# Borders between mixer and MLP in a four-layer fp32 trunk: norm root on other engines, combinations moved, out-projection reordered

## The chip, the cores and the metric

The kernel runs on one core of one Trainium2 chip. The metric is the device time in microseconds (us) of one execution. The kernel before has a median of 2815.55 us over 3 runs (2807.36 to 2817.22).

## The reference, cut to what matters

Four residual layers act on a stream of 528 positions of width 1024. The mixers are, in order, gated DeltaNet (layer 0), differential attention (layer 1), RG-LRU (layer 2) and DeltaNet again (layer 3). An MLP with squared ReLU stands behind each.

```
def rmsnorm(x, w):
    y = xf * lax.rsqrt(jnp.mean(xf * xf, axis=-1, keepdims=True) + EPS)
    return y * w

for layer in range(DEPTH):
    u = rmsnorm(h, norm_mix_w[layer])
    y = (gated_deltanet, diff_attention, rglru_block)[layer % 3](u, ...)   # ends in: o @ w_out
    h = h + keep * y
    u = rmsnorm(h, norm_mlp_w[layer])
    h = h + keep * (jnp.square(jax.nn.relu(u @ w1)) @ w2)
h = rmsnorm(h, final_norm_w)
```

## The kernel before, in words

**Layout.** The stream lies transposed: tile `h[d]` holds channels 128 d to 128 d + 127 on the partitions and 528 positions along the free axis, d = 0 to 7. A product takes two halves of 264 positions (256 where only the output positions are left).

**Precision.** Every fp32 operand of a large product is split in a high part `hi` and a rest `lo`, and three products of the 1-pass format are summed: hi·hi, hi·lo and lo·hi (`part`, L372). A weight tile of 1024 columns is split by `wsplit` (L296): ScalarE makes `hi` (L305); `lo` is either a VectorE subtraction (L307, mode "v") or ScalarE's negative of `hi` (L309) to which a DMA from the GpSimd queue adds the weight from HBM (L310, mode "d"). `LO_ENG` (L46) names the mode for the two tiles of a row of weights; a name that is not in it has "dd". Seven slots of the pool `wp` hold the split tiles, so a tile is made when an earlier one has been used up.

**The norm.** The weight-scaled stream is multiplied first and the factor 1/sqrt(mean square) is applied when a product leaves PSUM. `norm_sq` (L417) squares `h[d]` on ScalarE (L429) and adds it to `ssum` on GpSimd (d = 1 to 6) or VectorE (d = 7), L430. `norm_finish` (L435) sums over the partitions with TensorE (`ones`), takes mean and EPS on VectorE (L442), the power -1/2 on GpSimd (L444, tile `rt`), spreads it over the partitions with TensorE into PSUM, and copies it to `rb` on ScalarE (L450).

**The border from mixer to MLP.** `out_proj` (L600) multiplies the eight head outputs by the output weight and adds the result to `h[d]` (L612). For DeltaNet and attention it makes two passes over d: heads 0 to 3, then heads 4 to 7; before each pass `drain` waits until those heads have been emitted. In the last pass `mlp_prep` (L454) follows each d: two ScalarE passes (L461, L462), a VectorE rest (L463) and `norm_sq`. Then `mlp` (L575) opens two plain columns of the first MLP weight with the first seven d (`open`), finishes the norm, and calls `mlp_combine` (L467) for the four pairs of d: six VectorE subtractions (L477) and two ScalarE casts (L480, L483) each, which build the operands of a seven-product scheme used for the other columns (`w1_pair`, L530).

**PSUM.** Eight banks: 3 in the pool `d` (large products), 5 in the pool `c` (all else). `psd` (L273) hands some `d` requests to the pool `c` where `self.wide` says so.

**What sets the order.** Background work (heads, gates, scans) is written as generators, which `tick` advances between matmuls by a model time; `t_img` in `dn_core` (L876) is such a time, at which a head may use matrices that a DMA brings back. The program runs under `schedule_with_timeline_sim=True`: at compile time a planner orders each engine's instructions by its own cost estimates, with program order as the priority, and `keep_in_program_order` pins an instruction. On the chip every engine and queue runs its own list in order.

**Other lines touched.** `lru_scan` (L1159) begins with four square roots on ScalarE (L1162). `run` (L1254) ends with the final norm: L1273 multiplies eight tiles by `rb`, three on GpSimd and five on VectorE, and L1274 writes them out.

Of the kernel before, what the change touches and what calls it, by code (L numbers as in the profile page):

```python
# [11 lines left out]
AF = mybir.ActivationFunctionType  # L12
ALU = mybir.AluOpType
# [4 lines left out]
NT = 8  # L18
# [24 lines left out]

LATS = [1.7] * 8 + [1.1]

LO_ENG = {"w2": "vd", "lru_in": "vd", "lru_out": "vd", "lru_gate": "vd"}  # L46

PRODS = (11, 21, 2, 3, 4, 1, 22)
OUT_PARTS = {"dn_out": (4, 4), "da_out": (4, 4), "lru_out": (8,)}


def out_order(name):

    o, n0 = [], 0
    for n in OUT_PARTS[name]:
        o += [(d, k) for d in range(8) for k in range(n0, n0 + n)]
        n0 += n
    return o


def unit_list(layers=LAYERS):
# [85 lines left out]
class K:  # L147
    def __init__(self, ctx, tc, hT, wts, cols, bc, cst, onehot, relb, out, layers):
# [22 lines left out]
        self.rb = per([128, TP], "rb")  # L171
        self.ones = per([128, 1], "ones")
        self.half = per([128, 1], "half")
        self.nhalf = per([128, 1], "nhalf")
        self.NS, self.NL = 34, 7
        self.sp = pool("sp", bufs=self.NS)
# [16 lines left out]
        nc.vector.memset(self.ssum, 0.0)  # L193
        nc.vector.memset(self.ones, 1.0)
        nc.vector.memset(self.half, 0.5)
        nc.vector.memset(self.nhalf, -0.5)
        self.ident = self.cst[:, CST["ident"]:CST["ident"] + 128]
        self.dimg = [self.drp.tile([2 * NC * (CB + 1), CB], F32, name=f"dimg{i}", bufs=1) for i in range(2)]
# [218 lines left out]
    def norm_sq(self, d, dve=False):  # L417
        nc = self.nc
        a = self.t0
        if dve:  # L420
            i = self.getl()
            nc.vector.tensor_tensor(self.S(i), self.h[d], self.h[d], ALU.mult)
            (nc.vector if d > 4 else nc.gpsimd).tensor_tensor(self.ssum[:, :T], self.ssum[:, :T], self.S(i), ALU.add)
            return
        if d == 0:
            nc.scalar.activation(self.ssum[:, a:T], self.h[d][:, a:], AF.Square)
        else:
            i = self.getl()
            nc.scalar.activation(self.S(i)[:, a:], self.h[d][:, a:], AF.Square)  # L429
            (nc.vector if d == NT - 1 else nc.gpsimd).tensor_tensor(self.ssum[:, a:T], self.ssum[:, a:T], self.S(i)[:, a:], ALU.add)  # L430

    def us(self):
        return self.u

    def norm_finish(self):  # L435

        nc = self.nc
        ps = self.psc()
        for c in range(NC):
            self.mmul(ps[:C, c:c + 1], lhsT=self.ssum[:, c * C:(c + 1) * C], rhs=self.ones, start=True, stop=True)  # L440
        ms = self.small([C, NC], "ms")
        nc.vector.tensor_scalar(ms, ps[:C, :NC], 1.0 / D, EPS, ALU.mult, ALU.add)  # L442
        rt = self.small([C, NC], "rt")
        nc.gpsimd.tensor_tensor(rt, ms, self.nhalf[:C].broadcast_to([C, NC]), ALU.pow)  # L444
        for c0, m in GR:
            pb = self.psc()
            for c in range(m):
                self.mmul(pb[:, c * C:(c + 1) * C], lhsT=rt[:, c0 + c:c0 + c + 1].broadcast_to([C, 128]),
                                 rhs=self.ident[:C, :C], start=True, stop=True)
            nc.scalar.copy(self.rb[:, c0 * C:(c0 + m) * C], pb[:, :m * C])  # L450
        return rt


# [121 lines left out]
    def mlp(self, l, next_prep, early=None):  # L575
        nc = self.nc
        self.open([("w1p", l, 0), ("w1p", l, 1)], self.us(), NT - 1)
        self.norm_finish()
        for p in range(NT // 2):
            self.mlp_combine(p)  # L580
        G = 32 // HG
        for g in range(G):
            xs = [] if g else self.w1_plain(l)
            for f in range(0 if g else 2, HG, 2):
                xs += self.w1_pair(l, g * HG + f, f == HG - 2)
            if g == 1 and early:
                self.spawn(early())
            self.wide = (0, 2, 4, 5, 7)
            self.open([("w2", l, d, g) for d in range(2)], xs, HG - 2)
            for d in range(NT):  # L590
                def ev(ps, t0, w):
                    h = self.h[d][:, t0:t0 + w]
                    nc.vector.tensor_tensor(h, h, ps, ALU.add)  # L593

                self.mm(("w2", l, d, g), xs, ev)
                if g == G - 1:
                    next_prep(d)
            self.wide = None

    def out_proj(self, name, slot, xs, l, part=None):  # L600

        nc = self.nc
        order = out_order(name)
        parts = OUT_PARTS[name]
        if part is None:
            part = len(parts) - 1
        n0, n = sum(parts[:part]), parts[part]
        if part == len(parts) - 1:
            self.ut, self.U = [], []
        for d in range(NT):  # L610
            def ev(ps, t0, w):
                nc.vector.tensor_tensor(self.h[d][:, t0:t0 + w], self.h[d][:, t0:t0 + w], ps, ALU.add)  # L612

            ws = []
            for k in range(n0, n0 + n):
                j, i = divmod(order.index((d, k)), 8)
                if i == 0:
                    self.ow = self.unit((name, slot, j))
                ws.append(tuple(x[:, i * 128:(i + 1) * 128] for x in self.ow))
            self.mmu(ws, [tuple(self.R(a) for a in xs[k]) for k in range(n0, n0 + n)], ev)  # L620
            if part == len(parts) - 1:
                self.mlp_prep(d, l * 8)


    def conv(self, x, y, wname, base, step, bias=None):
# [21 lines left out]
    def deltanet(self, slot, l, last):  # L647
# [45 lines left out]
        for h in range(8):  # L693
# [2 lines left out]
            hi, lo = self.get(True), self.get(True)  # L696
            xs.append((hi, lo))
            gates.append(self.spawn(self.dn_gate(heads[h], z, t, hi, lo), 0.7))
        n = 0
        for p, k in enumerate(OUT_PARTS["dn_out"]):  # L700
            n += k
            self.drain(*gates[:n])
            self.out_proj("dn_out", slot, xs, l, p)
        self.lat = 1.6

    def dn_beta(self, slot, xba, beta, ngc, negc, gd, tri):
# [68 lines left out]
    def dn_core(self, slot, l, h, cv, st, beta, ngc, negc, gd, mneg, ba):  # L775
# [97 lines left out]
        TM, TT = self.L(TMi, CB), self.L(TTi, CB)  # L873
        nc.sync.dma_start(TM[:CB], img(im, 0))
        nc.sync.dma_start(TT[:CB], img(im, NC * (CB + 1) * CB))
        t_img = self.now + 4.0  # L876
        yield 0.2

        vti = self.getl()
# [138 lines left out]
    def diffattn(self, slot, l, last):  # L1018
# [13 lines left out]
        self.open([("da_in", slot, 0), ("da_in", slot, 8)], us, NT - 1)  # L1032
        self.norm_finish()
        xs, gens = [None] * 8, []
        for h in range(8):
            q, k, v = self.get(), self.get(), self.get()

# [4 lines left out]
            self.mm(("da_in", slot, 8 + h), us, self.evac_rb(self.S(k)))  # L1042
            self.mm(("da_in", slot, 16 + h), us, self.evac_rb(self.S(v)))
            gens.append(self.spawn(self.da_core(h, xs, q, k, v, self.vs, nlam), 0.5))
        n = 0
        for p, k in enumerate(OUT_PARTS["da_out"]):
            n += k
            self.drain(*gens[:n])
            self.out_proj("da_out", slot, xs, l, p)

    def da_tiles(self, ts, q, k, E, Em, vt, on, so, nlam):
        nc = self.nc
# [106 lines left out]
    def lru_scan(self, fs, hs, xr, sg):  # L1159
        nc = self.nc  # L1160
        for f in fs:
            nc.scalar.activation(self.S(hs[f][0]), self.S(hs[f][0]), AF.Sqrt, scale=0.0625)  # L1162
        yield 0.5
        for f in fs:
            tr, ti, a = hs[f]
# [88 lines left out]
    def run(self):  # L1254
# [8 lines left out]
        for i, (kind, slot, l) in enumerate(L):  # L1263
# [3 lines left out]
                self.mlp(l, lambda d: self.norm_prep(d, "mix", nxt), self.bias_vectors if L[i + 1][0] == 1 else None)  # L1267
            else:
                self.mlp(l, self.final_prep)
        self.norm_finish()  # L1270
        for d in range(NT):
            o = self.S(self.fin[d])[:, NM:]
            (nc.gpsimd if d % 3 == 1 else nc.vector).tensor_tensor(o, o, self.rb[:, NM:T], ALU.mult)  # L1273
            nc.sync.dma_start(self.out[:, d, :], o)  # L1274

    def final_prep(self, d):
        self.norm_sq(d)
# [10 lines left out]
def layout(i, layers=LAYERS):  # L1288
# [10 lines left out]
    for n, j, u in ((n, j, u) for n, us in enumerate(rows) for j, u in enumerate(us)):  # L1299
# [14 lines left out]
            dst[:] = blk(i["mlp_w1"][u[1]], 0, u[2])  # L1314
        elif u[0] == "w2":
            dst[:] = blk(i["mlp_w2"][u[1]], u[3], u[2])
        elif u[0] in OUT_PARTS:
            w = i[u[0][:-4] + "_w_out"][u[1]]
            for j, (d, k) in enumerate(out_order(u[0])[8 * u[2]:8 * u[2] + 8]):
                dst[:, j * 128:(j + 1) * 128] = w[k * 128:(k + 1) * 128, d * 128:(d + 1) * 128]  # L1320
# [42 lines left out]
```

## Time and profile before

| | |
|---|---|
| median of 3 runs | 2815.55 us |
| profiled execution: its own time | 2808.51 us |
| profiled execution: span, first to last instruction | 2806.7 us |
| TensorE (PE) busy | 2685.4 us, 96% of the span |
| VectorE (DVE), ScalarE (ACT), GpSimd (POOL) busy | 60%, 52%, 26% |
| mean granted TensorE clock | 0.976 of full speed |

TensorE sets the time: what can be saved is its idle time and the time for which it ran at the lower clock. A row of a timeline gives the start and the length in us and, in brackets, how long the engine stood idle before and what released it. PEclk is the granted clock as a share of full speed.

### The profile page before, as it was taken

To read this page: it belongs to the slowest core of one execution; us is meant where nothing else is said; L and a number is where in the kernel's file an instruction comes from. 1 tells how busy PE (TensorE), PEld (TensorE's weight loads), DVE (VectorE), ACT (ScalarE), POOL (GpSimd) and SP (SyncE) were. 2 spreads that over 40 slices of the span, in tenths; PEclk is the share of its full clock that TensorE was granted. 3 is DMA by queue.
4 is the path that set the end of the run, shared out by engine and by line. 5 is a ranking of instruction groups with operands and counts; after the bars stand their busy time and mean duration, and the time that the engine had idled before them with its cause. 6 is when DMAs were issued, how large, how long until landed. Compare 5 with 4: busy or idle time off the path is not lost.

```text
span 2806.7 us, 54609 instructions
## 1 busy us (share of the span) xinstructions
PE 2685.4 (96%) x22080; PEld 2606.7 (93%) x22080; DVE 1674.3 (60%) x3841; ACT 1461.1 (52%) x3024; POOL 720.2 (26%) x984
## 2 busy tenths in 40 slices
PE   7899999999999999999999999999999999899997
PEld 7899898999998887999999999999999988799997
DVE  5755447656734445776566766776376553567763
ACT  4566555444545555543456854444566564544443
POOL 2655522101121112111122121111236453311112
PEclk9999999999999999999999999999999999999998
DMA  7755453354465443343454434433677454344333
GB/s 200 161 124 119 87 134 92 99 162 134 130 145 124 100 105 91 104 123 106 121 148 124 128 97 122 143 106 100 161 166 161 101 112 99 83 136 128 121 98 106
DMA packets 128866, 343.84 MB, mean 123 GB/s; under 512 B 72789, under 2 KB 73213, under 8 KB 103397
## 3 DMA queue, kind: packets, MB, share of 16 engines
q10 hardware_dynamic: 38496, 212.61, 22.0%
q0 software_dynamic: 28224, 102.77, 21.2%
q1 hardware_dynamic: 61892, 24.96, 3.7%
q8 instruction: 173, 2.83, 0.4%
q14 instruction: 81, 0.66, 0.1%
HBM read 331.99 MB, written 11.01 MB: 122 GB/s over the span
## 4 chain that ended last, share of the span: by engine, by line
PE 78%; issue 6%; DMA 5%; DVE 4%; POOL 4%; ACT 3%; DVEq 0%; ACTq 0%; POOLq 0%; SPq 0%
PE d L218 41%; PE c L218 35%; DMA lo<-in_wts_dram 2%; PE c L222 2%; POOL rt L444 1%; DVE op L307 1%; DMA s<-dimg 1%; DMA s<-gd 1%; POOL s L863 1%; DMA sa<-s 1%; POOL s L864 1%; ACT lo L309 0%; DMA gd<-l 0%; DVE l L539 0%; DMA dimg<-s 0%
## 5 line engine op out<-in xcount | busy, mean ns | idle before, releaser
L218 PE MATMUL c<-s,hi 128*128 128x264 f32 (+1 forms) x2816 | 522.0, 284 | 0.1
L218 PE MATMUL d<-uh,hi 128*128 128x264 f32 (+1 forms) x1584 | 468.5, 296 | 10.2 <-DVE s L642 10.1
L218 PE MATMUL d<-s,hi 128*128 128x264 f32 (+1 forms) x2432 | 467.9, 289 | 7.9 <-ACT s L400 2.0
L218 PE MATMUL d<-ul,hi 128*128 128x264 f32 (+1 forms) x1584 | 462.8, 292 | 0.0
L218 PE MATMUL d<-uh,lo 128*128 128x264 f32 (+1 forms) x1584 | 461.9, 292 | 0.4 <-DMA lo<-in_wts_dram 0.4
L218 PEld LDWEIGHTS c<-s,hi 128*128 128x128 f32 x2816 | 435.9, 188 | 1.4 <-issue 1.1
L310 POOL DMA_DIRECT2D lo<-in_wts_dram x196 | 173.9, 887 | 982.7 <-ACT lo L309 696.3
L218 PEld LDWEIGHTS d<-s,hi 128*128 128x128 f32 x2432 | 385.1, 192 | 13.6 <-issue 2.3
L218 PE MATMUL c<-s,lo 128*128 128x264 f32 (+1 forms) x1408 | 394.6, 284 | 1.9 <-DMA lo<-in_wts_dram 1.7
L309 ACT ACTIVATE lo<-hi 128x1024 fp32r<-128x1024 f32 x196 | 207.7, 1060 | 351.1 <-PE d L218 244.2
L305 ACT CAST hi<-raw 128x1024 fp32r<-128x1024 f32 x278 | 288.0, 1041 | 127.4 <-PE c L218 78.8
L218 PE MATMUL d<-s,lo 128*128 128x264 f32 (+1 forms) x1216 | 349.4, 288 | 3.6 <-DMA lo<-in_wts_dram 3.5
L218 PEld LDWEIGHTS d<-uh,hi 128*128 128x128 f32 x1584 | 306.4, 193 | 19.2 <-DVE s L642 13.7
L218 PEld LDWEIGHTS d<-uh,lo 128*128 128x128 f32 x1584 | 305.5, 193 | 5.2 <-issue 3.2
L218 PEld LDWEIGHTS d<-ul,hi 128*128 128x128 f32 x1584 | 306.0, 193 | 2.6 <-issue 1.6
L305 ACT CAST op<-raw 128x512 fp32r<-128x512 f32 x300 | 180.9, 619 | 168.7 <-PE d L218 100.3
L218 PEld LDWEIGHTS c<-s,lo 128*128 128x128 f32 x1408 | 263.5, 188 | 3.4 <-DMA lo<-in_wts_dram 3.1
L307 POOL TENSOR_TENSOR op<-raw,op 128x512 fp32r<-128x512 f32 x60 | 114.8, 1913 | 546.7 <-ACT op L305 407.0
L218 PEld LDWEIGHTS d<-s,lo 128*128 128x128 f32 x1216 | 232.9, 192 | 5.9 <-DMA lo<-in_wts_dram 4.2
L218 PE MATMUL d<-s,op 128*128 128x264 f32 (+1 forms) x1716 | 228.2, 284 | 0.0
L218 PEld LDWEIGHTS d<-s,op 128*128 128x128 f32 x1716 | 216.4, 188 | 0.0
L593 DVE TENSOR_TENSOR h<-h,c 128x264 f32<-128x264 f32 (+1 forms) x172 | 73.1, 425 | 229.3 <-PE c L218 228.9
(260 smaller groups left out, 5577.8 us busy)
## 6 DMA issues: line engine op xcount, KB each, us to landing
raw<-in_wts_dram ACTq DMA_DIRECT2D x197, 1024.0 KB
lo<-in_wts_dram POOLq DMA_DIRECT2D x196, 512.0 KB, 5.9
s<-dimg SPq DMA_DIRECT2D x32, 245.0 KB
sa<-s SPq DMA_DIRECT2D x16, 245.0 KB
s<-gd ACTq DMA_DIRECT2D x14, 265.0 KB
vs<-vd SPq DMA_DIRECT2D x8, 327.5 KB
h<-in_hT_dram SPq DMA_DIRECT2D x8, 264.0 KB
s<-vs SPq DMA_DIRECT2D x8, 264.0 KB
```

Source lines behind the costliest of these rows:

```text
L218: return self.nc.tensor.matmul(out, lhsT=lhsT, rhs=rhs, start=start, stop=stop)
L222: return self.nc.tensor.transpose(out, in_, ident)
L305: nc.scalar.copy(hi, src)
L307: lo_eng.tensor_tensor(lo, src, hi.bitcast(F32), ALU.subtract)
L309: nc.scalar.activation(lo, hi.bitcast(F32), AF.Copy, scale=-1.0)
L310: nc.gpsimd.dma_start(lo, dram, accum_op=ALU.add)
L444: nc.gpsimd.tensor_tensor(rt, ms, self.nhalf[:C].broadcast_to([C, NC]), ALU.pow)
L593: nc.vector.tensor_tensor(h, h, ps, ALU.add)
L863: nc.gpsimd.tensor_tensor(t, bt[:, j, j + 1:, None].broadcast_to([NB, r, j]), X[:, None, j, :j].broadcast_to([NB, r, j]), ALU.mult)
L864: nc.gpsimd.tensor_tensor(X[:, j + 1:, :j], X[:, j + 1:, :j], t, ALU.subtract)
```

## The change

The root of the norm has a second form, taken at the four MLP borders: a square root on ScalarE, then reciprocal and one Newton step on VectorE. `mlp_combine` for pairs 0 to 2 is called inside `out_proj`. The steps of the out-projection follow a list: heads 0 to 3 for all d, heads 4 to 6 for d = 0 to 3, head 7 for d = 0 to 3, heads 4 to 7 for d = 4 to 7, with a drain up to the last head that a step uses. The square of d = 7 is taken in halves. The RG-LRU weights have both `lo` tiles on VectorE. Two of eight large products of the attention stage go to the pool `c`. The first head's `t_img` is 5.5 instead of 4.0. The first square root of each scan is pinned. At the end, six of eight tiles are multiplied straight from PSUM in two pieces, two on GpSimd.

```diff
-LO_ENG = {"w2": "vd", "lru_in": "vd", "lru_out": "vd", "lru_gate": "vd"}
+LO_ENG = {"w2": "vd", "lru_in": "vv", "lru_out": "vv", "lru_gate": "vv"}
-OUT_PARTS = {"dn_out": (4, 4), "da_out": (4, 4), "lru_out": (8,)}
+HEADS4 = [(d, 0, 4) for d in range(8)] + [(d, 4, 7) for d in range(4)] + [(d, 7, 8) for d in range(4)] + [(d, 4, 8) for d in range(4, 8)]
+OUT_STEPS = {"dn_out": HEADS4, "da_out": HEADS4, "lru_out": [(d, 0, 8) for d in range(8)]}
...
-            nc.scalar.activation(self.S(i)[:, a:], self.h[d][:, a:], AF.Square)
-            (nc.vector if d == NT - 1 else nc.gpsimd).tensor_tensor(self.ssum[:, a:T], self.ssum[:, a:T], self.S(i)[:, a:], ALU.add)
+            for t0, n in (self.hv if d == NT - 1 else ((a, T - a),)):
+                sl = slice(t0, t0 + n)
+                nc.scalar.activation(self.S(i)[:, sl], self.h[d][:, sl], AF.Square)
+                (nc.vector if d == NT - 1 else nc.gpsimd).tensor_tensor(self.ssum[:, sl], self.ssum[:, sl], self.S(i)[:, sl], ALU.add)
...
-    def norm_finish(self):
+    def norm_finish(self, root=False, out=None):
...
+        if root:
+            sq = self.small([C, NC], "sq")
+            nc.scalar.activation(sq, ps[:C, :NC], AF.Sqrt, scale=1.0 / D, bias=self.eps[:C])
+            nc.vector.tensor_scalar(ms, ps[:C, :NC], -0.5 / D, -0.5 * EPS, ALU.mult, ALU.add)
+            nc.vector.reciprocal(rt, sq)
+            nc.vector.tensor_tensor(sq, rt, rt, ALU.mult)
+            nc.vector.tensor_tensor(sq, sq, ms, ALU.mult)
+            nc.vector.scalar_tensor_tensor(rt, sq, 1.5, rt, ALU.add, ALU.mult)
+        else:
+            nc.vector.tensor_scalar(ms, ps[:C, :NC], 1.0 / D, EPS, ALU.mult, ALU.add)
+            nc.gpsimd.tensor_tensor(rt, ms, self.nhalf[:C].broadcast_to([C, NC]), ALU.pow)
...
+            if out is not None:
+                out.append((pb, c0 * C, (c0 + m) * C))
...
     def mlp(self, l, next_prep, early=None):
-        self.norm_finish()
-        for p in range(NT // 2):
-            self.mlp_combine(p)
+        self.norm_finish(True)
+        self.mlp_combine(NT // 2 - 1)
...
+    def out_proj(self, name, slot, xs, l, gens=()):
+        self.ut, self.U = [], []
+        n = 0
+        for d, k0, k1 in OUT_STEPS[name]:
+            self.drain(*gens[:k1])
...
+            self.mmu(ws, [tuple(self.R(a) for a in xs[k]) for k in range(k0, k1)], ev)
+            if k1 == 8:
+                self.mlp_prep(d, l * 8)
+                if d % 2 == 1 and d < NT - 1:
+                    self.mlp_combine(d // 2)
...
-        t_img = self.now + 4.0
+        t_img = self.now + (4.0 if h else 5.5)
...
+        self.wide = (0, 4)
         for h in range(8):
             q, k, v = self.get(), self.get(), self.get()
...
+        self.wide = None
+        self.out_proj("da_out", slot, xs, l, gens)
...
+            root = nc.scalar.activation(self.S(hs[f][0]), self.S(hs[f][0]), AF.Sqrt, scale=0.0625)
+            if f == fs[0]:
+                self.tc.keep_in_program_order(root)
...
-            o = self.S(self.fin[d])[:, NM:]
-            (nc.gpsimd if d % 3 == 1 else nc.vector).tensor_tensor(o, o, self.rb[:, NM:T], ALU.mult)
+            o = self.S(self.fin[d])
+            if d in (2, 5):
+                nc.gpsimd.tensor_tensor(o[:, NM:], o[:, NM:], self.rb[:, NM:T], ALU.mult)
+            else:
+                for pb, t0, t1 in pbs:
+                    nc.vector.tensor_tensor(o[:, max(t0, NM):min(t1, T)], o[:, max(t0, NM):min(t1, T)], pb[:, max(NM - t0, 0):min(t1, T) - t0], ALU.mult)
```

## Rows read from the trace of the kernel before

**Rows 1.** The page: busy time of each engine, share of the span, instructions
```profile
PE 2685.4 (96%) x22080; PEld 2606.7 (93%) x22080; DVE 1674.3 (60%) x3841; ACT 1461.1 (52%) x3024; POOL 720.2 (26%) x984
```

**Rows 2.** Waits of TensorE, whole span: engine, line, releaser; us in total, times, longest
```profile
PE c L218 <- POOL rt L444: 21.9, 5, 5.5
...
PE c L218 <- DMA s<-dimg: 13.5, 6, 4.1
...
PE c L218 <- DMA lo<-in_wts_dram: 8.3, 6, 2.6
```

**Rows 3.** Timeline of TensorE, first MLP border: start, us, line, operation, idle before
```profile
438.03 1.01 PE L218 MATMUL c<-ones,ssum 128*106 128x1 f32 x10
...
447.59 2.47 PE L218 MATMUL c<-cst,rt 106*128 106x106 f32 x10 [5.51 <-POOL rt L444]
```

**Rows 4.** Timelines of GpSimd and VectorE at the same border
```profile
439.69 7.85 POOL L444 TENSOR_TENSOR rt<-ms,nhalf 106x5 f32<-106x5 f32 x1 [10.85 <-DVE ms L442]
...
445.20 1.28 DVE L307 TENSOR_TENSOR op<-raw,op 128x512 fp32r<-128x512 f32 x2
```

**Rows 5.** Tile rt, the instructions that write it: ns min/median/max, first and last start
```profile
L444 POOL TENSOR_TENSOR rt<-ms,nhalf x9: 1188/1197/7848, 29.1 to 2791.4; 106x5 f32<-106x5 f32 x9
```

**Rows 6.** Windows behind two of the four border stalls: us, busy by engine, PEclk, DMA
```profile
1135.20:1142.20 7.00, 6.99 (x32) 6.99 (x33) 2.85 (x6) 2.72 (x6) 1.20 (x1) 0.51 0.00 0
...
2452.70:2459.70 7.00, 7.00 (x46) 7.00 (x47) 4.25 (x9) 4.08 (x10) 1.15 (x1) 0.76 0.23 57
```

**Rows 7.** Groups by line: ScalarE, VectorE in 404 to 438 us, then GpSimd, VectorE, whole span
```profile
L461 ACT ACTIVATE s<-h,cols 128x528 f32<-128x528 f32 x8 | 5.9, 738 | 8.4 <-DVE h L612 8.4
...
L462 ACT CAST uh<-s 128x528 fp32r<-128x528 f32 x8 | 5.0, 619 | 0.0
...
L612 DVE TENSOR_TENSOR h<-h,d 128x264 f32<-128x264 f32 x16 | 6.7, 426 | 14.7 <-PE d L218 14.6
...
L463 DVE TENSOR_TENSOR ul<-s,uh 128x528 fp32r<-128x528 f32 x8 | 7.5, 934 | 0.7 <-ACT uh L462 0.7
...
L477 DVE TENSOR_TENSOR l<-s,l 128x264 f32<-128x264 f32 x4 | 1.5, 427 | 0.0
...
L477 DVE TENSOR_TENSOR s<-l,s 128x528 fp32r<-128x528 f32 x24 | 16.3, 700 | 0.0
...
L820 DVE RECIPROCAL cj<-nk 106x5 f32<-106x5 f32 x16 | 2.9, 182 | 0.1
...
L430 POOL TENSOR_TENSOR ssum<-ssum,l 128x528 f32<-128x528 f32 (+1 forms) x51 | 69.4, 1361 | 94.4 <-ACT l L429 88.2 <-DVE ssum L423 4.6 <-DVE h L593 1.5
```

**Rows 8.** Waits of TensorE and windows where the mixers of layers 1 and 3 end
```profile
PE d L218 <- ACT s L1140: 1.5, 1, 1.5
...
1087.70:1097.70 10.00, 7.53 (x31) 6.84 (x32) 4.09 (x11) 3.65 (x6) 1.33 (x2) 0.50 0.06 18
...
PE c L222 <- DVE l L984: 2.8, 1, 2.8
...
PE d L218 <- ACT s L400: 2.0, 1, 2.0
...
2404.40:2412.40 8.00, 5.69 (x26) 4.97 (x27) 2.64 (x9) 3.32 (x6) 1.28 (x1) 0.57 0.00 0
```

**Rows 9.** Layer 2: a wait (1580 to 1640 us); groups of ScalarE and VectorE, whole span
```profile
PE d L218 <- DMA lo<-in_wts_dram: 2.8, 1, 2.8
...
L309 ACT ACTIVATE lo<-hi 128x1024 fp32r<-128x1024 f32 x196 | 207.7, 1060 | 351.1 <-PE d L218 244.2 <-PE c L218 105.4 <-DVE l L570 0.8
...
L307 DVE TENSOR_TENSOR lo<-raw,hi 128x1024 fp32r<-128x1024 f32 x82 | 101.9, 1244 | 28.5 <-PE d L218 9.0 <-PE c L218 6.9 <-ACT hi L305 6.6
...
L1162 ACT ACT_TABLE_LOAD x8 | 10.3, 1283 | 0.1
```

**Rows 10.** Waits of TensorE in the attention stage, 850 to 1070 us
```profile
PE d L218 <- DVE s L642: 4.4, 5, 0.9
```

**Rows 11.** Timeline of VectorE at the end of the kernel
```profile
2795.53 6.30 DVE L1273 TENSOR_TENSOR s<-s,rb 128x512 f32<-128x512 f32 x5 [4.20 <-ACT rb L450]
```
## What was predicted before the change was run

> **What bounds the kernel now.** I read the page first. TensorE is busy for 2685.4 us of the span of 2806.7 [rows 1], so it is the bound, and at most the 121 us of its idle time, plus what it loses at the lower clock, can be had. Its 22080 matmuls in 2685.4 us make 0.122 us each. Second came the view of its waits [rows 2]. The largest is for `rt`, the power -1/2 on GpSimd: 21.9 us in five waits. Then come 13.5 us for the images of the DeltaNet heads (`dimg`) and 8.3 us for weight rests (`lo`) that a DMA completes.
>
> Third, the timelines of the first MLP border. The sums over partitions start at 438.03 us; TensorE then has work until 442.08, and waits 5.51 us for `rt` [rows 3]. The power itself starts at 439.69 and takes 7.85 us [rows 4], though the same instruction takes 1.2 us in the median of nine [rows 5]. Why? VectorE's unbroken stream of combinations and weight rests ends at 446.48 (445.20 + 1.28), and the power ends 1.06 us after that, at 447.54 [rows 4]. So the power was held up by VectorE's stream and ran once that stopped. At the MLP borders of layers 1 to 3 the picture repeats.
>
> Behind each of these waits the granted clock is at its lower level, 1.2 GHz, for a while: in the 7 us after it, in which TensorE is busy throughout, PEclk is 0.51 in one border and 0.76 in another, with the other two between [rows 6]. Time at half clock loses half of itself, so 7 us x (1 - PEclk) is lost: 3.4 to 1.7 us, about 2.55 per border.
>
> **The change, part by part.** Minus is gained; the sum stands against the profiled execution's 2808.5 us.
>
> 1. *Root at four MLP borders.* The power leaves GpSimd and cannot be held up there. Of the 21.9 us, the fifth wait is at the end of the kernel, and its power stays: I leave it 1.2 us [rows 5]. Idle gained: 20.7 us; clock: 4 x 2.55 = 10.2. Together -30.9. The new chain is a square root of 5 elements and four dependent VectorE instructions of 0.18 us each, for which the reciprocal stands [rows 7]: about 1.5 us with handovers. TensorE's work after the sums covers 3.0 us (439.04 to 442.08) [rows 3], so the chain costs nothing in itself while the sums come no later. The square root needs a table load of 1.283 us, as those of layer 2 do [rows 9]; it lies ahead of the wait for the sums, with ScalarE idle, and I cost it at nothing (if uncovered: 1.3 us per border).
>
> 2. *Earlier combinations, later second pass.* No instruction is added but eight evacuations per reordered border (8 x 0.43 us on VectorE [rows 7]), yet the work crowds. In DeltaNet and attention all `mlp_prep` now come after head 7's step at d = 0. From there TensorE needs 24 matmuls for head 7, 96 for d = 4 to 7 and 84 for the two opened columns: 204 x 0.122 = 25 us. In that time ScalarE has eight times 0.74 + 0.62 + 0.62 (a square costs about what a cast does) = 15.8, six casts of the combinations 3.7, and splits of the next weights, two passes of 1.06 for each of two tiles and three casts of half tiles at 0.62: 6.1; 25.6 in all. VectorE has 16 evacuations (6.8), eight rests at 0.7 to 0.93 (5.6 to 7.5), three combinations at 4 x 0.43 + 2 x 0.70 = 3.1 (9.3), and seven weight rests and sums at 0.7, 4.9 [rows 7, 9]: 27 to 29. The pair is about as long as its cover. Bounds for the sums' delay: nothing, or 3 us idle with 1.7 us of clock behind. I take 2 us at three borders and 0.5 in layer 2, where the steps stay spread out: +6.5.
>
> 3. *First MLP weights.* Their `lo` is three serial steps: ScalarE, a place in GpSimd's queue behind the additions to `ssum`, a DMA. Today TensorE waits for it at three of the openings (among the 8.3 us, the longest 2.6 [rows 2]). The crowd of part 2 is ahead of it on both queues. Bounds: these waits go, or grow by 4 us each; I take +2 at each of three, clock included: +6.
>
> 4. *End of the mixers.* In layer 1 TensorE waits for the last attention head four times, 1.5 us and three of 1.1 to 1.2, 5.0 in sum, and runs at PEclk 0.50 for 10 us, of which it is busy 7.53 [rows 8]: 3.8 us lost. In layer 3 it waits 2.8 and 2.0 us; PEclk 0.57 over 8 us is 6.9 us at the lower level, less 2.3 idle, half of the rest 2.3 [rows 8]. Sum 15.9. The new order gives head 7 the time of 72 more matmuls, 8.8 us, more than these waits. Layer 0 has next to none. Eight short tiles then follow, each 0.37 us of TensorE against 0.43 of evacuation, with three banks: I leave 2.4 us for that. -13.5 (bounds: -15.9 and 0).
>
> 5. *RG-LRU weights.* 14 rests go from ScalarE's negative (1.06 us) and a DMA to VectorE (1.24 us) [rows 9]. The 2.8 us wait ahead of the out-projection goes, with the smallest clock loss of rows 6: -4.5. VectorE's 17 us more lie in a stage where it has room (60% busy over the span [rows 1]). Eight square roots with eight table loads [rows 9] should need fewer once the first is pinned; ScalarE is not the bound there, and a pinned instruction can also hold its queue: nothing, bounds -3 to +3.
>
> 6. *Images.* `t_img` of the first head, 1.5 us later in two layers, lets other matmuls go first. Of the 13.5 us, one wait is 4.1 [rows 2]. -3 (bounds 0 and -6).
>
> 7. *Attention in more PSUM.* Five waits, 4.4 us, for evacuations by VectorE [rows 10]; a fourth bank in four products should absorb most, while heads get less of pool `c`: -3 (bounds -4.4, +2).
>
> 8. *Final factors.* VectorE waits for the copy to `rb` [rows 11]; the first piece can start a copy and a group of broadcasts earlier, and GpSimd has two products instead of three: -1.2 (bounds 0, -2).
>
> Sum: -30.9 + 6.5 + 6 - 13.5 - 4.5 - 3 - 3 - 1.2 = -43.6, so 2764.9 on the profiled scale. The median of the three runs is 7.0 us above the profiled execution; I add that: **2772 us**, 1.5% below 2815.55.
>
> On part 1 the Trainium skill is stricter, page "ScalarE: Activation LUTs", section "What ACT_TABLE_LOAD costs": a switch of table set costs about 2.66 us, a drain included. An estimate from that page: 1.4 us more per border, 5.5 in all, if it were uncovered. The trace's load is 1283 ns [rows 9], and I hold to the row.
>
> **Rivals.**
>
> *A. The hold-up moves instead of going.* What held the power can hold GpSimd's six additions per border too, 1.36 us each in the mean [rows 7], and the weight DMAs queued behind them: the combinations that made VectorE's stream now run right beside these additions. The price of one hold-up is the power's, 7.85 - 1.2 = 6.65 us [rows 4, 5]. Three held additions are 20 us, less the 3 us cover, plus 2.55 of clock: 19.5 per border, 78 in all in place of the 30.9 removed, that is +47 against -25 from parts 4 to 8. With +22 and the offset it gives 2837, slower. It decides from 2.2 held additions per border, where 4 x 14 us make up for both gains. Against it: evacuations read one operand from PSUM and break the stream, and before the border additions ran while VectorE's rests stretched (0.93 in the mean against 0.70 for the same size [rows 7]). Chance 0.08.
>
> The Trainium skill speaks for A, page "SBUF — State Buffer", section "Who interferes with whom": a VectorE instruction with two SBUF inputs and a GpSimd instruction that reads SBUF exclude each other, and the second to start waits in full. By that rule, the trace agrees: the power ended 1.06 us after the stream [rows 4].
>
> *B. Backlog.* ScalarE and VectorE become the bound of the border: 3 us idle and 1.7 of clock at four borders (+19), weights +4 at three and their clock 1.5 (+16.5), parts 4 to 8 at -21: -16, with the offset 2799; with a weaker backlog 2790. For it: the totals of part 2. Against: today both engines are idle for long there. Chance 0.22.
>
> *C. Short steps.* `mlp_prep` and combinations get between the eight evacuations, 12 us of VectorE against 2.9 of TensorE: 9 us idle and 3 of clock at three borders, +36: 2808, no change. Against: the first combination waits for ScalarE, so evacuations go ahead. Chance 0.10.
>
> *D. The root isn't what holds TensorE* (another releaser ends the wait at once): parts 4 to 8 alone, 2808.5 - 25 + 7 = 2790. Part of the same interval; chance 0.05.
>
> **How the numbers follow.** Forecast 0.55, A 0.08, B 0.22, C 0.10, D 0.05. About 0.5% (14 us) is what a measurement of this kernel can tell from no change; slower than 2801.5 is not faster. All best ends at once (no delay in part 2, the three waits of part 3 gone, 6.6 us) give -73, or 2742; that all of them come is unlikely, and I begin at 2746. On the other side the range goes to 2803: it takes in B and D and leaves out A and most of C. Faster: forecast, D and four fifths of B, 0.78. Same: the rest of B and most of C, 0.15. Slower: 0.07.
>
> **What would show it.** Right: no wait for `rt` at the MLP borders, PEclk 1.00 in the 7 us behind; no wait for the last head's lines in layers 1 and 3; no `lo` wait at the LRU out-projection; square-root loads at the borders ahead of ScalarE's idle time. Wrong: waits for `ssum`, for `lo` at the openings or for L612's successor of several us each (B, C), or GpSimd additions of several us (A).

## The result, and the profile after

The changed kernel takes 2781.24 us (median of 4 runs, 2776.89 to 2785.95) against 2815.54 us in the same set (4 runs, 2807.36 to 2817.22). The ratio is 0.9884, with a 95% interval of 0.9859 to 0.9910: faster by 1.2%, or 34.3 us. The forecast was 2772, the range 2746 to 2803. The profiled execution of the changed kernel took 2785.95 us, the slowest of the four, and that of before 2808.51, near the fastest of its set. So the two traces lie only 22.6 us apart, and what follows reads stages, not only spans.

The page first: TensorE is as busy as before [rows 1], with as many matmuls; GpSimd is busy for 28.9 us less (a power that is held up counts as busy) and VectorE for 35.5 more.

```profile
PE 2683.2 (96%) x22080; PEld 2603.7 (94%) x22080; DVE 1709.8 (61%) x3911; ACT 1460.2 (52%) x3029; POOL 691.3 (25%) x965
```

The waits of TensorE over the whole span (engine, line, releaser; us in total, times, longest). L456 is the power that stays, L448 to L453 the new root, L491 and L477 the old L477 and L463, L655 the old L642, L1147 the old L1140.

```profile
PE c L218 <- DMA s<-dimg: 11.1, 4, 4.7
PE d L218 <- ACT s L400: 10.3, 2, 8.3
...
PE c L218 <- DMA lo<-in_wts_dram: 5.8, 5, 1.9
PE d L218 <- DMA lo<-in_wts_dram: 5.1, 5, 2.0
...
PE d L218 <- ACT s L1147: 2.4, 2, 1.5
...
PE c L218 <- DVE ul L477: 2.2, 3, 1.1
...
PE c L218 <- POOL rt L456: 1.5, 1, 1.5
```

Where [rows 2] had 21.9 us for `rt`, 1.5 is left, at the end of the kernel. No MLP border waits for the norm any more. But a new wait of 8.3 us has come, for `s` of L400, the RG-LRU output on its way to the out-projection.

The timeline of VectorE at the first border (start, us) shows the new chain, in place of the 7.85 us of [rows 4]:

```profile
442.20 0.15 DVE L449 TENSOR_SCALAR ms<-c 106x5 f32<-106x5 f32 x1
442.27 0.17 DVE L450 RECIPROCAL rt<-sq 106x5 f32<-106x5 f32 x1
442.37 0.38 DVE L491 TENSOR_TENSOR l<-s,l 128x264 f32<-128x264 f32 x1
442.68 0.15 DVE L451 TENSOR_TENSOR sq<-rt 106x5 f32<-106x5 f32 x1
442.79 0.43 DVE L491 TENSOR_TENSOR l<-s,l 128x264 f32<-128x264 f32 x1
443.14 0.16 DVE L452 TENSOR_TENSOR sq<-sq,ms 106x5 f32<-106x5 f32 x1
443.33 0.17 DVE L453 SCALAR_TENSOR_TENSOR rt<-sq,rt 106x5 f32<-106x5 f32 x1
```

It takes 1.3 us, with two pieces of a combination in between. On TensorE the broadcasts start at 444.50, without a wait, where [rows 3] had 447.59. Windows of 7 us behind the broadcasts of the four borders (us; busy us of PE, PEld, DVE, ACT, POOL; PEclk, the granted clock; DMA share and GB/s) show PEclk 1.00, against 0.51 and 0.76 in [rows 6]:

```profile
447.00:454.00 7.00, 7.00 (x60) 7.00 (x59) 7.00 (x16) 4.77 (x10) 0.21 (x1) 1.00 0.46 150
1137.00:1144.00 7.00, 7.00 (x60) 7.00 (x59) 7.00 (x15) 5.11 (x10) 0.61 (x1) 1.00 0.45 151
1675.00:1682.00 7.00, 7.00 (x60) 7.00 (x59) 6.88 (x15) 5.42 (x11) 0.96 (x1) 1.00 0.44 150
2438.00:2445.00 7.00, 7.00 (x62) 7.00 (x61) 7.00 (x15) 4.71 (x11) 0.00 (x0) 1.00 0.46 153
```

To see where the time went, I cut each trace at the starts of the nine sums over partitions (the `ones` matmuls, whose starts stand in the trace). An MLP stage runs from the sums ahead of it to the next, and so holds the border's wait for `rt`. DN is DeltaNet, LRU is RG-LRU, and the first 28 us are left out. Lengths in us, one execution each, from starts read to 0.1 us; the experiments' rows are explained below. Kernels with the same code in a stage still differ there by some us (DeltaNet of layer 0: 409.7 after, 405.6 without the fourth bank), so a difference counts for more where it repeats.

| kernel | DN 0 | MLP 0 | attn | MLP 1 | LRU | MLP 2 | DN 3 | MLP 3 | end | span |
|---|---|---|---|---|---|---|---|---|---|---|
| before | 410.2 | 366.8 | 321.8 | 363.9 | 175.0 | 362.5 | 415.8 | 346.1 | 16.8 | 2806.7 |
| after | 409.7 | 360.9 | 330.0 | 360.5 | 179.5 | 355.8 | 406.8 | 336.8 | 15.6 | 2783.8 |
| root only | 412.1 | 366.1 | 328.5 | 363.8 | 176.2 | 361.8 | 418.0 | 347.8 | 16.7 | 2818.8 |
| moved only | 411.7 | 358.3 | 319.0 | 356.8 | 174.9 | 356.1 | 415.8 | 337.8 | 16.7 | 2775.3 |
| moved, root | 411.2 | 358.3 | 322.6 | 358.9 | 175.0 | 355.6 | 415.1 | 338.7 | 16.8 | 2780.1 |
| moved, order | 407.8 | 361.9 | 320.0 | 361.2 | 176.3 | 355.6 | 410.5 | 339.1 | 16.8 | 2778.2 |
| after, not moved | 409.1 | 367.6 | 322.5 | 365.5 | 179.6 | 360.2 | 405.4 | 345.7 | 14.6 | 2798.8 |
| after, two passes | 417.5 | 357.8 | 327.0 | 358.5 | 179.8 | 354.3 | 411.4 | 341.6 | 15.7 | 2792.2 |
| after, no fourth bank | 405.6 | 360.7 | 322.8 | 359.9 | 180.2 | 356.5 | 410.3 | 336.7 | 15.6 | 2776.1 |
| selection | 405.5 | 360.3 | 322.5 | 357.2 | 175.1 | 355.6 | 406.5 | 339.6 | 14.3 | 2764.5 |

The four MLP stages are shorter by 5.9 + 3.4 + 6.7 + 9.3 = 25.3 us and DeltaNet of layer 3 by 9.0; RG-LRU is longer by 4.5, attention by 8.2.

### The profile page after: what moved, and what is told of

It reads as the page before. It is cut to its first block, busy times and chain, and to the rows that moved or that the text cites. A ratio compares the mean times of both kernels' runs of the same rounds, so it can differ in the third digit from the quotient of the medians.

```text
span 2783.8 us, 54631 instructions
## 1 busy us (share of the span) xinstructions
PE 2683.2 (96%) x22080; PEld 2603.7 (94%) x22080; DVE 1709.8 (61%) x3911; ACT 1460.2 (52%) x3029; POOL 691.3 (25%) x965
## 5 line engine op out<-in xcount | busy, mean ns | idle before, releaser
L218 PE MATMUL d<-uh,hi 128*128 128x264 f32 (+1 forms) x1496 | 444.0, 298 | 7.5 <-DVE s L655 7.5
L218 PE MATMUL d<-uh,lo 128*128 128x264 f32 (+1 forms) x1496 | 439.6, 294 | 2.7 <-DMA lo<-in_wts_dram 2.7
L218 PE MATMUL d<-ul,hi 128*128 128x264 f32 (+1 forms) x1496 | 437.2, 292 | 0.0
L310 POOL DMA_DIRECT2D lo<-in_wts_dram x182 | 161.7, 889 | 901.1 <-ACT lo L309 586.1
L309 ACT ACTIVATE lo<-hi 128x1024 fp32r<-128x1024 f32 x182 | 192.9, 1060 | 332.4 <-PE d L218 200.5
L218 PEld LDWEIGHTS d<-uh,hi 128*128 128x128 f32 x1496 | 290.8, 195 | 15.1 <-DVE s L655 9.4
L218 PEld LDWEIGHTS d<-uh,lo 128*128 128x128 f32 x1496 | 290.0, 194 | 7.9 <-DMA lo<-in_wts_dram 3.6
L218 PEld LDWEIGHTS d<-ul,hi 128*128 128x128 f32 x1496 | 290.4, 194 | 1.8 <-issue 1.0
L307 POOL TENSOR_TENSOR op<-raw,op 128x512 fp32r<-128x512 f32 x60 | 121.9, 2031 | 585.0 <-ACT op L305 399.6
```

The source lines that it names most:

```text
L218: return self.nc.tensor.matmul(out, lhsT=lhsT, rhs=rhs, start=start, stop=stop)
L307: lo_eng.tensor_tensor(lo, src, hi.bitcast(F32), ALU.subtract)
L309: nc.scalar.activation(lo, hi.bitcast(F32), AF.Copy, scale=-1.0)
L310: nc.gpsimd.dma_start(lo, dram, accum_op=ALU.add)
```

## The experiments

The theory to test was the forecast's: the root takes the power off GpSimd, and that is what opens the border. The first rival was that something else ends the wait at once (D of the forecast). All ratios are to the kernel before, timed in the same set, with a 95% interval.

**1. The root alone.** The kernel before with the root's form added, and with this:

```diff
-        self.norm_finish()
+        self.norm_finish(True)
         for p in range(NT // 2):
             self.mlp_combine(p)
```

> The kernel before with the new root alone at the four MLP borders; combinations stay behind the norm. Theory H (the power on GpSimd was held up by VectorE's stream, and taking it off GpSimd is what pays): no wait for rt at the borders, 20 to 30 us under the kernel before, 2786 to 2796. Rival M (the moved combinations are what pays): TensorE gets past rt and then waits for the combinations instead, several us at each border; no more than 10 us under the kernel before.

Measured: 2811.32 us, ratio 1.0002 (0.9989 to 1.0015). The root gains nothing. VectorE's timeline at the first border, from that run (a square root on ScalarE was ready at 441.9):

```profile
441.99 0.18 DVE L450 RECIPROCAL rt<-sq 106x5 f32<-106x5 f32 x1
442.08 0.39 DVE L491 TENSOR_TENSOR l<-s 128x264 f32<-128x264 f32 x1
442.43 1.33 DVE L491 TENSOR_TENSOR s<-l,s 128x528 fp32r<-128x528 f32 x2
443.68 1.50 DVE L491 TENSOR_TENSOR l<-s,s 128x264 f32<-128x264 f32 x1
445.10 0.15 DVE L451 TENSOR_TENSOR sq<-rt 106x5 f32<-106x5 f32 x1
...
447.34 0.15 DVE L452 TENSOR_TENSOR sq<-sq,ms 106x5 f32<-106x5 f32 x1
...
449.58 0.15 DVE L453 SCALAR_TENSOR_TENSOR rt<-sq,rt 106x5 f32<-106x5 f32 x1
```

The four small steps are 0.15 to 0.18 us each, as forecast, but combinations and weight rests stand between them: 7.7 us from the first to the end of the last. That is the power's 7.85 [rows 4] over again, in VectorE's own order. TensorE then shows the old wait under a new name (timeline of TensorE at this border, then its waits over the whole span, same run):

```profile
449.88 2.44 PE L220 MATMUL c<-cst,rt 106*128 106x106 f32 x10 [5.90 <-DVE rt L453]
...
PE c L220 <- DVE rt L453: 13.1, 3, 6.6
PE d L220 <- DVE s L491: 5.6, 3, 2.2
```

The waits for `rt` stay long in layers 0 and 3. In layer 1 only 0.6 us of them is left and in layer 2 none, but there TensorE waits for the combinations instead (L491, and 1.8 us for their casts, L494). In sum that is 20.5 us at the borders, against 20.4 before. The order in VectorE's queue is the planner's; whether the root alone would pay with its four small steps pinned together was not tried.

**2. The moved combinations alone.** The kernel before, power on GpSimd, one edit:

```diff
     def mlp(self, l, next_prep, early=None):
...
-        for p in range(NT // 2):
-            self.mlp_combine(p)
+        self.mlp_combine(NT // 2 - 1)
...
     def out_proj(self, name, slot, xs, l, part=None):
...
                 self.mlp_prep(d, l * 8)
+                if d % 2 == 1 and d < NT - 1:
+                    self.mlp_combine(d // 2)
```

> The kernel before with one edit: the combinations of pairs 0 to 2 called inside the last pass of the out-projection; power on GpSimd, two passes, all else as before. Theory M (taking the combinations out of VectorE's stream behind the sums is what frees the border, with either root): the power under 3 us and no more than 2 us of waits for rt per border; 12 to 22 us under the kernel before. Theory H as first put (the root's engine decides): under 6 us.

Measured: 2777.95 us, ratio 0.9888 (0.9869 to 0.9906). One edit of a few lines gives what the whole change gives, and more than the 12 to 22 us that were expected. The tile `rt` in that run (ns min/median/max), against a maximum of 7848 in [rows 5]:

```profile
L444 POOL TENSOR_TENSOR rt<-ms,nhalf x9: 1190/1202/1591, 29.5 to 2760.0; 106x5 f32<-106x5 f32 x9
```

The power stayed where it was and is held up for a fraction of a microsecond at most, since VectorE's stream is over sooner. At the first border it starts at 442.17 and takes 1.59 us, and VectorE has one piece of a combination left (timeline of VectorE, that run):

```profile
442.01 0.70 DVE L477 TENSOR_TENSOR s<-l,s 128x528 fp32r<-128x528 f32 x1
443.83 1.75 DVE L307 TENSOR_TENSOR op<-raw,op 128x512 fp32r<-128x512 f32 x1 [1.12 <-ACT op L305]
```

TensorE's waits for `rt` are 1.9 us over the whole span, and PEclk is 1.00 in the 7 us behind the broadcasts of all four borders. The MLP stages shrink by 8.5 + 7.1 + 6.4 + 8.3 = 30.3 us.

**3. The power kept, in the changed kernel** (`self.norm_finish()` in `mlp` again; all else as after).

> The changed kernel with the power on GpSimd at the MLP borders again; the combinations of three pairs stay in the out-projection. Theory H: the stream that VectorE still has after the sums (from 439 to 447 us in the first border) holds the power up again; it takes 4 us or more, TensorE waits 2 to 5 us for rt at each border, 12 to 25 us over the changed kernel. Rival M: with three of four combinations gone from behind the sums the power takes about 1.2 us and the time is within 5 us of the changed kernel.

Measured: 2783.08 us, ratio 0.9897 (0.9880 to 0.9913), beside the 0.9884 of after: no difference that can be measured. The power takes 1.2 to 2.6 us at the borders, and TensorE never waits for it there.

**4. The root on top of the moved combinations** (experiments 1 and 2 together; two passes, all else as before).

> The kernel before with the combinations moved (as in e5) and the root at the four MLP borders; two passes, all else as before. Theory that the root adds nothing once the stream is short: the same as e5, 2775 to 2781 us, with no wait for rt over 1 us at a border. Rival, that the root's chain of VectorE steps queues behind the moved combinations where there are two passes (as the waits for rt of 4.3 us in e3 suggest): 2783 to 2793 us, MLP stages 2 to 4 us longer each than in e5.

Measured: 2781.88 us, ratio 0.9895 (0.9878 to 0.9913), beside 0.9888 for experiment 2. The median lies 0.9 us above the theory's range and 1.1 us below the rival's. The stages speak against the rival: each MLP stage is at most 2.1 us longer. One wait for `rt` of L453 is left, 1.9 us, where the theory had none over 1 us.

**5. The changed kernel without the move.**

```diff
-        self.mlp_combine(NT // 2 - 1)
+        for p in range(NT // 2):
+            self.mlp_combine(p)
...
-                if d % 2 == 1 and d < NT - 1:
-                    self.mlp_combine(d // 2)
```

> The changed kernel with the combinations of pairs 0 to 2 back behind the norm in the MLP; the root, the new order and all else stay. Theory that the moved combinations carry the border's gain: it goes again, about 7 us per border, with waits for rt at the borders written by VectorE (as in the run of the root alone), 2800 to 2812 us, ratio 0.995 to 1.000. Rival, that in the changed kernel the order of the output steps has taken over part of it (the evacuations and casts come later, so VectorE's stream is cut up anyway): 2785 to 2795, with waits for rt of under 2 us.

Measured: 2799.15 us, ratio 0.9956 (0.9939 to 0.9973), so some 20 us of the 34 go by the ratios (0.9956 against 0.9884). The MLP stages are 6.7 + 5.0 + 4.4 + 8.9 = 25.0 us longer than after. That is the theory's size and ratio; the median lies 0.85 us below its range, and all six executions (from 2796.25) lie above the rival's 2795. Waits of TensorE in that run:

```profile
PE c L218 <- DVE rt L453: 14.9, 3, 7.2
```

With the root in place, the wait for the norm comes back as soon as the combinations do.

**6. Two passes in the changed kernel** (the new order undone, root and move kept).

```diff
-HEADS4 = [(d, 0, 4) for d in range(8)] + [(d, 4, 7) for d in range(4)] + [(d, 7, 8) for d in range(4)] + [(d, 4, 8) for d in range(4, 8)]
+HEADS4 = [(d, 0, 4) for d in range(8)] + [(d, 4, 8) for d in range(8)]
```

> The changed kernel with the out-projection of DeltaNet and attention in two passes again (heads 0 to 3, then 4 to 7, for all d), combinations still after each odd d. Prediction's part 4 (72 matmuls cover the last head): 10 to 15 us over the changed kernel. Theory S (the last head slips by as much as the matmuls put before it take, so nothing is gained): within 5 us of the changed kernel, or under it, with the last attention head's cast some 10 us earlier after the start of the stage.

Measured: 2792.87 us, ratio 0.9927 (0.9910 to 0.9943), some 12 us more than after, within the 10 to 15 expected; the intervals touch. The loss lies in the DeltaNet stages (+7.8 and +4.6 us); attention is 3.0 us shorter and the MLP stages 1.8 in sum. The last attention head's cast comes 6.7 us earlier after the stage's start. TensorE has two waits for `rt` of L453, 4.3 us in sum.

**7. The order on top of the moved combinations** (experiment 2 with the new list of steps; power, LRU, attention products and the rest as before).

> The kernel before with the combinations of pairs 0 to 2 moved (as in e5) and the new order of the output steps in DeltaNet and attention; the power stays on GpSimd. Theory that the order pays by itself: the last heads get 9 us more at the ends of layers 1 and 3, so about 8 us less than e5's 2778, near 2770 us (ratio 0.985). Rival, that the order pays only where the root relieves VectorE's queue or GpSimd: like the changed kernel, 2781, or worse. Rival 2, that in layer 1 the head only slips by what it is given: attention stage about 327 us against 319 in e5 and no gain there, DeltaNet of layer 3 about 406 against 416, in sum near 2776 us.

Measured: 2779.42 us, ratio 0.9885 (0.9866 to 0.9904): nothing against experiment 2, nearest to the first rival. The stages tell why. The two DeltaNet stages get shorter by 3.9 and 5.3 us, attention gains nothing (+1.0), and the four MLP stages take back 3.6 + 4.4 - 0.5 + 1.3 = 8.8. At the first border TensorE now waits for the last operands (waits, 425 to 470 us of this run):

```profile
PE c L215 <- DVE ul L460: 2.1, 3, 1.0
PE c L215 <- ACT uh L459: 0.7, 1, 0.7
```

So the order pays in experiment 6 and not here. Root, combinations and two passes alone (experiment 4) show no loss, so it isn't the root and two passes either; which of the other parts makes two passes dear was not tried.

**8 to 10. The RG-LRU.** Three variants of the changed kernel: `lo` by ScalarE and a DMA again; no square root pinned; all four roots of each scan pinned.

```diff
-LO_ENG = {"w2": "vd", "lru_in": "vv", "lru_out": "vv", "lru_gate": "vv"}
+LO_ENG = {"w2": "vd", "lru_in": "vd", "lru_out": "vd", "lru_gate": "vd"}
```
```diff
-            if f == fs[0]:
-                self.tc.keep_in_program_order(root)
```
```diff
-            if f == fs[0]:
-                self.tc.keep_in_program_order(root)
+            self.tc.keep_in_program_order(root)
```

> The changed kernel with the RG-LRU weight rests half on VectorE and half by DMA again, as before. Prediction's part 5: the wait for a DMA of 2.8 us is back and 4 to 5 us are lost against the changed kernel. Theory G (what ends the RG-LRU stage is the chain of the last scan and gelu on ScalarE and VectorE; the weight wait only lay ahead of it): within 3 us of the changed kernel, the wait for the last split shorter by what the weight wait takes. Third: VectorE's 14 rests more made that chain late, then 4 us or more under the changed kernel.

> The changed kernel without the pin on the first square root of each scan. Prediction's part 5: no difference, within 3 us. Rival (the pin holds ScalarE's queue and makes the last scan late): 4 us or more under the changed kernel, with the wait of TensorE ahead of the RG-LRU out-projection under 5 us.

> The changed kernel with all four square roots of each scan pinned, not only the first. Theory G (the stage ends with the chain of the last scan on ScalarE, in which two table loads of 1.28 us and a cast lie between the third and the fourth square root): square roots follow one another, some 8 table loads fewer, the wait of 8.3 us ahead of the out-projection 3 us or less, 4 to 8 us under the changed kernel. Rival (ScalarE is not what makes the chain late, or the pins hold gates and evacuations up): no gain, or 3 us over it.

Measured: 2783.72 us (0.9898, 0.9880 to 0.9916), 2779.62 (0.9884, 0.9865 to 0.9903) and 2787.40 (0.9907, 0.9891 to 0.9923). No total differs surely from after, but together with the kernel before and experiment 2 the stages make a square (LRU stage; wait for `s` of L400 ahead of the out-projection):

| | no root pinned | first root pinned |
|---|---|---|
| `lo` by a DMA | 175.0 us; none (2.8 for `lo`) | 183.5 us; 4.8 (7.4 for `lo`) |
| `lo` on VectorE | 177.0 us; 2.6 | 179.5 us; 8.3 |

In these traces, one for each corner, the pin makes the stage longer in both rows. The other kernels agree with two of the corners: 174.9 to 176.3 us in the five that have both as before, 179.6 to 180.5 in the four that have both as after. The timeline of ScalarE in the changed kernel, ahead of the wait:

```profile
1607.60 0.64 ACT L1184 ACTIVATE s<-s 128x528 f32<-128x528 f32 x1 [2.20 <-DVE s L655]
1608.26 1.28 ACT L1169 ACT_TABLE_LOAD   x1
1609.55 0.64 ACT L1169 ACTIVATE s<-s 128x528 f32<-128x528 f32 x1
1610.21 1.28 ACT L1188 ACT_TABLE_LOAD   x1
1611.51 0.64 ACT L1188 ACTIVATE s<-s 128x528 f32<-128x528 f32 x1
1613.54 2.24 ACT L400 CAST s<-s 128x528 fp32r<-128x528 f32 x4 [1.39 <-DVE s L1194]
```

and TensorE's next row, `d<-s,hi`, waits for that cast:

```profile
1614.22 1.33 PE L218 MATMUL d<-s,hi 128*128 128x264 f32 x4 [8.28 <-ACT s L400]
```

The last root and its table loads stand in the chain that TensorE waits for. But loads aren't the whole of it: with all four pinned, loads for the roots in this stretch fall from four to one, and the wait for L400 is still 6.0 us, now behind one scan's four roots in a row. That stage takes 182.4 us, and the kernel, which was to be 4 to 8 us under after, is 6 us over it. What else delays the chain is open.

**11. No fourth bank for the attention products** (`self.wide = (0, 4)` left out of the changed kernel).

> The changed kernel without the attention stage's use of pool c for large products. Prediction's part 7: 3 us over the changed kernel, with waits of TensorE for evacuations of about 4 us back. Rival (heads lose PSUM banks and the last head comes later): under the changed kernel by 3 us or more, the attention stage shorter.

Measured: 2775.42 us, ratio 0.9868 (0.9851 to 0.9886). Waits of TensorE in the attention stage, first after (844 to 1064 us):

```profile
PE d L218 <- DVE s L655: 1.4, 3, 1.0
PE d L218 <- DMA lo<-in_wts_dram: 1.0, 1, 1.0
```

then without the fourth bank (840 to 1060 us), where the 4.4 us of [rows 10] are back:

```profile
PE d L218 <- DVE s L655: 4.4, 5, 0.9
```

The fourth bank takes 3.0 us of waits away, and the kernel is no faster for it. The rival fits better: without the bank the median is 5.8 us under after, the attention stage takes 322.8 us instead of 330.0, and the last head's cast comes 4.1 us earlier after the stage's start. The intervals of the two kernels overlap, but the stage mostly repeats: it takes 327.0 to 330.0 us in six of the seven traces with the bank, and 319.0 to 322.8 in six of the seven without. The exceptions are 322.5 with it (experiment 5) and 328.5 without it (experiment 1).

**12. A selection.** Moved combinations; the new order in DeltaNet alone; `t_img` of 5.5 for the first head; final factors from PSUM. The power, the RG-LRU and the attention products as before.

> The parts that seemed to pay, together: the combinations moved, the new order in DeltaNet alone, the first head's images 1.5 us later, the final factors from PSUM; the power on GpSimd, the RG-LRU weights, the attention products and the square roots of the scan as before. Theory that stage gains add up: MLP stages as in e5, DeltaNet stages 405 and 406, attention 319, RG-LRU 175, tail 15.6, which is 2765 us (ratio 0.983). Rival, that each gain in the DeltaNet stages is one of the schedule as a whole and doesn't carry over: 2776 us, as e5.

Measured: 2770.17 us (2766.30 to 2771.66), ratio 0.9854 (0.9832 to 0.9877). The interval overlaps with that of after, but the four executions lie below all four of after (from 2776.89) and all five of experiment 2 (from 2775.49). Most stages came as expected, DeltaNet 405.5 and 406.5, LRU 175.1, end 14.3; attention took 322.5 us instead of 319, and the median lies midway between the theory's 2765 and the rival's 2776. In these executions it is faster than both kernels.

## Why the prediction was right or wrong

The time was right to 9 us, and the range held it. The main step was wrong in its cause.

**Part 1, "The power leaves GpSimd and cannot be held up there": failed.** That VectorE's stream held the power was right: with the stream shorter the same instruction on the same engine takes 1.2 to 1.59 us (experiment 2). But the step credited the gain to the root, and the root alone gains nothing (experiment 1). The chain was priced at "about 1.5 us with handovers", as if VectorE were free. It goes into the very stream that held GpSimd up, and in experiment 1 its four dependent small steps were spread over 7.7 us of that stream. Rival D said so (another releaser ends the wait at once), with a chance of 0.05, for the root by itself. What paid was the edit that part 2 costed as a loss. The size, 20.7 of idle and 10.2 of clock, was right: experiment 2's MLP stages are 30.3 us shorter, against the 30.9 of the sum. The table load, costed at nothing, is over before the sums start in layers 1 and 2, and before they end in layer 3. In layer 0 it runs from 440.22 to 441.51, behind the sums (437.90 to 438.91), and TensorE's broadcasts still start without a wait.

**Parts 2 and 3, crowding and first weights: mis-sized, and tied to the wrong edit.** I had +12.5; the MLP stages of after are 5.0 us longer than experiment 2's. Such a loss came with the order in experiment 7 (+8.8 in MLP stages), but in the whole change two passes take only 1.8 us off these stages (experiment 6), so what makes up the 5.0 is open. At the first border TensorE waits 3.0 us for the last operands (2.2 for L477, 0.8 for their casts). The weights' waits at the openings didn't grow: 1.9 us in layer 1, 1.5 in layer 3, none in layers 0 and 2.

**Part 4, end of the mixers, -13.5: failed.** The step counted 72 more matmuls ahead of head 7; nine of its pass stood there before, so 63 are new, 7.7 us. They didn't free TensorE of the wait: the last head's cast came 298.2 us after the stage's start instead of 285.4. Two edits share in that. The order on top of experiment 2 moves the cast from 285.4 to 289.6 us; in the changed kernel two passes give 291.5, and the order without the fourth bank 294.1. The waits for the heads there are 3.6 us in sum (2.4 + 1.2) against 5.0. Windows of the changed kernel ahead of and in that stretch:

```profile
1072.00:1082.00 10.00, 9.08 (x66) 7.52 (x64) 4.01 (x20) 5.72 (x19) 1.95 (x2) 0.99 0.60 158
1082.00:1092.00 10.00, 9.57 (x37) 7.79 (x38) 4.44 (x17) 1.98 (x11) 1.87 (x2) 0.50 0.01 2
```

In layer 3 the two waits of [rows 8] are 1.7 (L993, the old L984) and 2.0 us instead of 2.8 and 2.0. Put on the moved combinations alone, the order shortens DeltaNet and lengthens the MLP by as much (experiment 7). Within the whole change it is worth some 12 us (experiment 6), near the size forecast, but against a loss that some other part brings where the order is missing. So its worth depends on what stands beside it, and it was no term to be summed by itself. What repeats is DeltaNet: layer 0, to which the step gave next to nothing, takes 403.7 to 409.7 us in the nine traces with the order there and 410.2 to 417.5 in the five without, and layer 3 takes 404.4 to 410.5 against 411.4 to 418.0.

**Part 5, RG-LRU, -4.5: failed.** The 2.8 us wait for `lo` [rows 9] went, and 8.3 us for L400 came: +4.5 in the stage. "A pinned instruction can also hold its queue" was the right thought, though its bound of 3 us was too small for one of the two rows of the square (8.5 and 2.5 us). The eight table loads, which the pin was to make fewer, stayed eight.

**Part 6, images.** The waits are 11.1 us against 13.5, but 14.3 in the selection, which has the edit too. It wasn't tried by itself and stays open.

**Part 7, attention products, -3: the wait went, the time did not** (experiment 11). That "heads get less of pool `c`" was priced at 2 us at most; the stage with the bank is 7.2 us longer, with the last head 4.1 us later. That the banks are what delays the heads is argued, not shown.

**Part 8, -1.2: right.** The end is 15.6 us instead of 16.8. The row that answers to [rows 11] (timeline of VectorE):

```profile
2774.15 4.06 DVE L1288 TENSOR_TENSOR s<-s,c 128x302 f32<-128x302 f32 x12 [3.44 <-ACT rb L462]
```

**Rivals.** A didn't come: the 51 additions to `ssum` on GpSimd take 1.33 us in the median and 1.86 at most, about as before (mean 1.36, [rows 7]). C didn't: TensorE waits for L622, the old L612, three times in the whole span, 0.6 us at most. B came in its weak form at most: in 1100 to 1165 us VectorE is busy for 63.26 of 65 us, but TensorE's waits there are 1.9 us for a weight and 0.4 for L622.

That the total came out well is partly luck: of what parts 4, 5 and 7 were to bring, 21 us, little or nothing is to be seen beside the kernel with the moved combinations alone, but the crowding and the weights cost less than half of the 12.5 us. Of the 34 us, that one edit gives 34 by itself; the rest of the change nets nothing.

## What to carry to other kernels

When a small operation is late because another engine's stream holds it, ask what ends the stream before asking where the small operation could go; moving it into the stream keeps the wait. A step that removes a wait is not worth that wait until the next releaser in the queue is named, and a reordering that shortens one stage must be booked together with the stage behind it. Run the smallest edit by itself: one of a few lines carried the gain of this change, and another, the pin, went with a longer stage.

## What was not expected of the hardware

The hold-up between VectorE and GpSimd goes both ways. In experiment 1 VectorE's piece of a combination that takes 0.39 to 0.43 us elsewhere took 1.50, at 443.68 to 445.18, while GpSimd ran a weight rest (timeline of GpSimd, that run):

```profile
443.52 1.36 POOL L309 TENSOR_TENSOR op<-raw,op 128x512 fp32r<-128x512 f32 x1 [13.68 <-ACT op L307]
```

It ends 0.30 us after GpSimd's instruction, which ends at 444.88. In experiment 2 it happened again: the VectorE row at 443.83 took 1.75 us, where the same instruction takes 0.68 at 445.52 in experiment 1, while GpSimd ran a weight rest from 443.75 to 445.03. In the Trainium skill, page "SBUF — State Buffer", section "Who interferes with whom", the engine that issues first has the shared ports and the other waits; by that rule, the trace agrees in both directions. Rival A reckoned with one direction alone.

The clock went down without long idle: in the second window above TensorE was busy for 9.57 of 10 us at PEclk 0.50, which is 1.2 GHz, and in the ten before it, at 0.99, for 9.08.
